# The last eight adaLN parts of a two-layer decoder: from scaling and summing to matmuls against the condition

## The chip, the cores and the metric

The kernel runs on one core of one Trainium2 chip. The metric is device time in microseconds (us) from launch to end on that core. A core has five engines that run side by side, each through its own queue in order: TensorE (PE, with its weight loads shown as PEld), VectorE (DVE), ScalarE (ACT), GpSimd (POOL) and SyncE (SP, which here only issues DMAs).

## The reference, cut to what matters

A decoder trunk of two layers over 512 tokens of 1024 features. Layer 0 mixes tokens by sparse attention, layer 1 by a gated linear recurrence (HGRN2); each mixer is followed by a mixture of 16 experts. Every one of the four sub-layers is modulated by a condition vector `c`: one product of silu(c), 1024 numbers, with a 1024 x 3072 matrix gives it a shift, a scale and a gate of 1024 numbers each.

```
cond = jax.nn.silu(c)
for layer in range(DEPTH):
    mod = jnp.einsum('bd,sde->sbe', cond, ada_w[layer]) + ada_b[layer][:, None, :]
    shift, scale, gate = jnp.split(mod[0], 3, axis=-1)
    h = rms_norm(x, norm_g[layer, 0]) * (1.0 + scale[:, None, :]) + shift[:, None, :]
    y = nsa_mixer(h, ...) if layer % 2 == 0 else hgrn2_mixer(h, ...)
    x = x + gate[:, None, :] * y
    shift, scale, gate = jnp.split(mod[1], 3, axis=-1)
    h = rms_norm(x, norm_g[layer, 1]) * (1.0 + scale[:, None, :]) + shift[:, None, :]
    x = x + gate[:, None, :] * hier_moe(h, ...)
```

All is float32. The four matrices of `ada_w` are 12 MB each, and are read once.

## The kernel before

**The parts.** `ada_parts(l, s)` cuts the matrix of a sub-layer into six parts of 512 columns, so there are 24 in all, numbered 6 * (2l + s) + t. A part is loaded as one tile `w` of 128 partitions x 8 slices x 512 columns (2 MB, line 91). Slice k holds rows 128k to 128k+127 of the matrix, and `cond[:, k]` holds the condition for them, one number for each partition. Parts 0 to 15 (`POOLED = 16`) are done on PE: for each slice and each quarter g of the columns one matmul with `cond[:, k]` spread over 32 columns as weights, into rows 32g to 32g+31 of one PSUM tile `ada_ps` (line 185). Eight such matmuls (two slices, four quarters) are one piece; the helper `side_by_side` raises the priority of all but the first and ties each to the one before, so that the scheduler queues a piece without a break. After each piece the generator yields.

Parts 16 to 23 go another way. Line 192 lets ACT multiply each of the eight slices by its condition, in place; line 198 lets POOL add the halves of the tile, 2048, 1024 and 512 columns wide; and line 202 lets PE sum over the partitions, with four matmuls against ones. Parts 16 and 17 are the gate of the HGRN2 mixer, parts 18 to 23 shift, scale and gate of the second mixture. Behind either way DVE takes the result out of PSUM (line 206 for a gate, line 209 for the others, which PE then transposes on line 211).

**The second mixer.** `hgrn` normalizes the tokens and runs `proj_stream` over eight weight tiles, called tile 0 to 7 here. ACT and DVE split each into a rounded part and a remainder (`whi`, `wlo`, lines 310 and 311) and PE multiplies: 96 matmuls of 512 columns for each tile (lines 337 to 339 and 341 to 343, `pr_ps`), the bulk of the stage. The split of the next tile happens during the last quarter of the current one. Between these matmuls the recurrence of eight heads is threaded (`hgrn_levels`, lines 1031 to 1088): nine levels, and at each PE multiplies small blocks of `Q` and `K` (`lvA_ps` to `lvD_ps`, lines 1043 to 1073), then DVE updates `Q` and `K` in place (lines 1080 and 1081), and the next level's matmuls need that. `hgrn_rest` closes a head (`ho_ps`, `ho_tp`). Only behind the last head comes the output projection (`out_ps`, lines 373 to 375) with its own two weight tiles, split on lines 313 and 314, and behind it the second mixture.

**What sets the order.** The code is traced by generators: `merge` advances the parts by 0.45 of a step (`HADA`) for each step of the heads, and `advance` the stream by 1.25 steps (`HSTREAM`). The framework's scheduler then orders the instructions of each engine, at build time, by priority and its own estimates; on the chip each engine takes them strictly in that order and waits where one is not ready. Weight tiles and parts share a ring of two buffers (`ring`, `RING = 2`): a load waits on its queue, SP's for most and POOL's for the first ones, until the tile two loads earlier is used up. The PSUM tiles of `mm_ps` (three buffers) are shared by `pr_ps`, `ada_ps` and `ho_ps`.

Of the kernel before, what the change touches and what calls it, by code (L numbers as in the profile page):

```python
# [13 lines left out]
AF = mybir.ActivationFunctionType  # L14
ALU = mybir.AluOpType
# [5 lines left out]
NK = D // 128  # L21
# [8 lines left out]
RING = 2  # L30
RINGB = 4
EARLY = 3
POOLED = 16
ADDED = 1

PARTS = ((0, 1, 2), (3,))
PINNED = (13, 14, 15)
# [25 lines left out]
def kernel(ctx: ExitStack, tc: tile.TileContext, I, out, dbg=None, upto="all"):  # L63
    nc = tc.nc
# [11 lines left out]
    def mm_ps(name):  # L76
        return psum.tile([128, 512], F32, tag="mm", bufs=3, name=name)

    def tp_ps(name):
        return psum.tile([128, 512], F32, tag="tp", bufs=3, name=name)  # L80
# [8 lines left out]
    def load_w(src, pool=ring, eng=nc.sync):  # L89
        w = pool.tile([128, 8, 512], F32, tag="w", name="w")  # L90
        loads.append(eng.dma_start(out=w, in_=src))
        return w
# [28 lines left out]
    with sb("init") as init:  # L121
# [16 lines left out]
        cond = const.tile([128, 8], F32, name="cond")  # L138
# [3 lines left out]
    def edge(ins, other, sync=False):  # L142
        tc.add_manual_dep(ins.ins, other.ins.name,
                          mybir.DependencyInfo(mybir.DependencyClass.Sync if sync else mybir.DependencyClass.NoSync,
                                               mybir.DependencyReason.DATA), reason="side by side")

    def side_by_side(makes):

        first = last = makes[0]()
        for make in makes[1:]:  # L150
            with tc.high_priority(offset=TOGETHER):
                ins = make()
            edge(ins, last)
            last = ins
        return first
# [5 lines left out]
    onef = const.tile([128, 1], F32, name="onef")  # L161
    nc.gpsimd.memset(onef, 1.0)

    def ada_parts(l, s):

        aw = I["ada_w"][l, s]
        mod = const.tile([128, 16], F32, name=f"mod{l}{s}")
        gg = const.tile([128, 2, 128], F32, name=f"gg{l}{s}")
        mods[l, s] = mod
        gates[l, s] = gg  # L170

        def load(t, wpool, eng):
            if t == 4:
                nc.gpsimd.memset(gg, 0.0)
                nc.scalar.dma_start(out=gg[0:128:32],
                                    in_=bass.AP(tensor=I["ada_b"].tensor,
                                                offset=I["ada_b"].offset + 3 * D * (2 * l + s) + 2 * D,
                                                ap=[[128, 4], [512, 2], [1, 128]]))
            return load_w(aw[:, 512 * t:512 * t + 512].rearrange("(k p) n -> p k n", p=128), wpool, eng)

        def part(t, w):
            if 6 * (2 * l + s) + t < POOLED:
                ps = mm_ps("ada_ps")
                for q in range(0, NK, 2):
                    side_by_side([lambda k=k, g=g: nc.tensor.matmul(
                        ps[32 * g:32 * g + 32, 0:128], cond[:, k:k + 1].to_broadcast([128, 32]),
                        w[:, k, 128 * g:128 * g + 128], start=(k == 0), stop=(k == NK - 1))
                        for k in (q, q + 1) for g in range(4)])
                    yield
            else:  # L190
                for k in range(NK):
                    nc.scalar.activation(w[:, k], w[:, k], AF.Copy, scale=cond[:, k:k + 1])  # L192
                    if k % 2:
                        yield
                n = NK
                while n > ADDED:
                    n //= 2
                    nc.gpsimd.tensor_tensor(w[:, 0:n], w[:, 0:n], w[:, n:2 * n], op=ALU.add)  # L198
                ps = mm_ps("ada_ps")
                for k in range(n):  # L200
                    for g in range(4):
                        nc.tensor.matmul(ps[32 * g:32 * g + 32, 0:128], onef.to_broadcast([128, 32]),
                                         w[:, k, 128 * g:128 * g + 128], start=(k == 0), stop=(k == n - 1))
                yield
            if t >= 4:
                nc.vector.tensor_add(gg[:, t - 4], gg[:, t - 4], ps[:, 0:128])
                return
            row = small.tile([128, 128], F32, tag="adarow", bufs=2, name="adarow")
            nc.vector.tensor_copy(row, ps[:, 0:128])
            tp = tp_ps("ada_tp")  # L210
            nc.tensor.transpose(tp[:, 0:128], row, ident)
            b0 = (2 * l + s) * 24 + 4 * t
            m4 = mod[:, 4 * t:4 * t + 4]
            nc.vector.tensor_add(m4, tp[:, 0:128:32], cols[:, b0:b0 + 4])
            if t >= 2:
                g0 = 96 + (2 * l + s) * 8 + 4 * (t - 2)
                nc.vector.scalar_tensor_tensor(m4, m4, 1.0, cols[:, g0:g0 + 4], op0=ALU.add, op1=ALU.mult)

        return [(lambda wpool=ring, eng=nc.sync, t=t: load(t, wpool, eng), lambda w, t=t: part(t, w)) for t in range(6)]

    def in_turn(parts, ahead, wpool=ring):
# [1545 lines left out]
```

## Time and profile before

| | us |
|---|---|
| median of 3 runs | 1475.61 |
| lowest and highest | 1474.67, 1477.06 |
| the profiled execution, own time | 1478.35 |
| its span, first to last instruction | 1476.5 |
| PE busy (share of the span) | 1291.1 (87%) |
| DVE busy | 723.1 (49%) |
| ACT busy | 468.1 (32%) |
| POOL busy | 225.5 (15%) |
| mean granted clock of PE, in parts of full speed | 0.944 |

Times inside a profile are counted from the first instruction. The span is 1.85 us shorter than the execution's own time, and the profiled execution is 2.74 us longer than the median. Busy times are unions of the instructions' own times; an engine that waits is not busy. [...] A matmul of 32-bit numbers stands as two instructions in the profile, as does its weight load.

### The profile page before, as it was taken

Reading aid. Unit: us, or ns where it says so; the run is one execution under the profiler, and the core shown is the slowest. Engines: PE = TensorE matmul, PEld = TensorE weight load, DVE = VectorE, ACT = ScalarE, POOL = GpSimd, SP = SyncE. Lnnn points to the kernel's source line nnn. Section 1 sums busy time; section 2 is a strip of 40 time slices with the busy share of each in tenths; the row PEclk is TensorE's granted clock in tenths of the full one; section 3 lists DMA queues with packets and bytes.
Section 4 is the critical chain, followed back from the end, with each engine's and each line's share of the span. In section 5 each row is a group of like instructions: output and inputs, shape, how many; then the busy total and the mean of one; then the engine's idle time right before and its main releaser. Section 6 shows DMA issues by size and latency. Waiting matters only on the chain. (4 is left out here: it accounts for less than half of the span.)

```text
span 1476.5 us, 25266 instructions
## 1 busy us (share of the span) xinstructions
PE 1291.1 (87%) x10122; PEld 767.6 (52%) x10123; DVE 723.1 (49%) x1791; ACT 468.1 (32%) x1071; POOL 225.5 (15%) x198
## 2 busy tenths in 40 slices
PE   4998899988989699999983998888979699999983
PEld 3776555765558333333323866566767543333330
DVE  2636886468854722222217476777665641222213
ACT  2523555336533211111115434344533121111110
POOL 1202212222100100000014025222130100000002
PEclk9999999999999799999996999999989799999997
DMA  9702552634564899999986222433338699999995
GB/s 354 206 11 85 176 185 91 252 121 152 192 265 157 282 368 343 376 381 334 384 325 182 86 103 87 157 115 115 115 115 299 235 343 365 360 377 335 367 397 193
DMA packets 168733, 346.42 MB, mean 235 GB/s; under 512 B 17236, under 2 KB 40620, under 8 KB 168605
## 3 DMA queue, kind: packets, MB, share of 16 engines
q1 hardware_dynamic: 135984, 276.80, 52.6%
q0 software_dynamic: 10560, 38.54, 8.0%
q10 hardware_dynamic: 22060, 29.34, 6.0%
q8 instruction: 84, 1.38, 0.4%
q14 instruction: 45, 0.36, 0.1%
HBM read 320.73 MB, written 23.93 MB: 233 GB/s over the span
## 5 line engine op out<-in xcount | busy, mean ns | idle before, releaser
L1452 PE MATMUL h_ps<-w,hgt 128*32 128x256 f32 (+1 forms) x2240 | 332.9, 488 | 0.0
L1452 PEld LDWEIGHTS h_ps<-w,hgt 128*32 128x32 f32 (+1 forms) x2240 | 111.8, 123 | 203.1 <-issue 172.4
L1479 PE MATMUL y_ps<-w,gT 128*32 128x256 f32 (+1 forms) x1120 | 163.6, 499 | 2.5 <-ACT gT L1468 2.1
L1458 DVE TENSOR_TENSOR g<-h_ps,g 32x256 f32<-32x256 f32 (+1 forms) x70 | 38.9, 556 | 253.7 <-ACT g L1456 253.1
L1456 ACT ACTIVATE g<-h_ps 64x512 f32<-64x512 f32 (+1 forms) x52 | 26.8, 516 | 368.2 <-PE h_ps L1452 346.2
L337 PE MATMUL pr_ps<-whi,hThi 128*128 128x512 f32 x288 | 119.6, 417 | 1.8 <-DVE qn L498 1.8
L338 PE MATMUL pr_ps<-wlo,hThi 128*128 128x512 f32 x288 | 115.6, 401 | 0.3 <-DVE wlo L311 0.3
L339 PE MATMUL pr_ps<-whi,hTlo 128*128 128x512 f32 x288 | 115.7, 402 | 0.2 <-DVE hTlo L283 0.2
L1479 PEld LDWEIGHTS y_ps<-w,gT 128*32 128x32 f32 (+1 forms) x1120 | 54.9, 125 | 97.3 <-issue 81.3
L1482 DVE TENSOR_TENSOR y<-y_ps,gate 128x512 f32<-128x512 f32 (+1 forms) x52 | 31.1, 598 | 123.3 <-PE y_ps L1479 107.5
L311 DVE TENSOR_TENSOR wlo<-w,whi 128x512 fp32r<-128x512 f32 x120 | 79.7, 702 | 23.0 <-ACT whi L310 22.8
L310 ACT ACTIVATE whi<-w 128x512 fp32r<-128x512 f32 x120 | 70.8, 629 | 39.0 <-SPq L1589 14.2
L782 ACT ACTIVATE P<-P,nm 128x128 f32<-128x128 f32 (+3 forms) x128 | 70.9, 556 | 36.9 <-DVE nm L780 35.8
L1416 POOL DMA_INDIRECT hg<-xnd,gidxp x26 | 23.7, 913 | 384.8 <-PE hg_tp L1428 383.0
L776 PE MATMUL s_ps<-kT,qT 128*128 128x256 f32 (+3 forms) x256 | 64.8, 358 | 12.0 <-DVE qn L498 6.9
L198 POOL TENSOR_TENSOR w<-w 128x2048 f32<-128x2048 f32 (+2 forms) x24 | 67.0, 2792 | 47.3 <-ACT w L192 46.1
L780 DVE CUSTOM_DVE_ANT_0 P<-s_ps,tb 128x128 f32<-128x128 f32 (+3 forms) x128 | 59.5, 485 | 21.5 <-PE s_ps L776 18.8
L1436 DVE TENSOR_SCALAR hgt<-hg_tp,mod 128x96 f32<-128x96 f32 (+2 forms) x128 | 43.7, 365 | 41.9 <-PE hg_tp L1428 36.4
L337 PEld LDWEIGHTS pr_ps<-whi,hThi 128*128 128x128 f32 x288 | 55.6, 193 | 15.1 <-issue 3.3
L339 PEld LDWEIGHTS pr_ps<-whi,hTlo 128*128 128x128 f32 x288 | 55.4, 192 | 12.2 <-DVE hTlo L283 0.4
L338 PEld LDWEIGHTS pr_ps<-wlo,hThi 128*128 128x128 f32 x288 | 55.9, 194 | 11.0 <-DVE wlo L311 0.7
L821 PE MATMUL p_tp<-ident,P 128*128 128x128 f32 x320 | 52.8, 282 | 8.2 <-DVE P L796 7.9
(361 smaller groups left out, 2121.9 us busy)
## 6 DMA issues: line engine op xcount, KB each, us to landing
w<-in_moe_w_dram SPq DMA_DIRECT2D x120, 1024.0 KB, 9.7
w<-in_moe_w_dram SPq DMA_DIRECT2D x32, 2048.0 KB, 9.5
w<-in_ada_w_dram SPq DMA_DIRECT2D x22, 2048.0 KB, 9.3
w<-in_hgrn_w_in_dram SPq DMA_DIRECT2D x12, 1024.0 KB, 6.9
tb<-tabd ACTq DMA_DIRECT2D x16, 456.0 KB, 3.8
yd<-y ACTq DMA_DIRECT2D x56, 128.0 KB, 5.0
w<-in_nsa_w_in_dram SPq DMA_DIRECT2D x3, 2048.0 KB, 8.1
yd<-zero POOLq DMA_DIRECT2D x12, 512.0 KB, 9.6
```

The source lines that it names most:

```text
L198: nc.gpsimd.tensor_tensor(w[:, 0:n], w[:, 0:n], w[:, n:2 * n], op=ALU.add)
L310: nc.scalar.activation(a, w[:, k], AF.Copy)
L311: nc.vector.tensor_sub(b, w[:, k], a.bitcast(F32))
L337: nc.tensor.matmul(ps, hi[:, k, c], a, start=(k == 0), stop=False)
L338: nc.tensor.matmul(ps, hi[:, k, c], b, start=False, stop=False)
L339: nc.tensor.matmul(ps, lo[:, k, c], a, start=False, stop=(k == NK - 1))
L776: nc.tensor.matmul(sp[:, :n], qT[:, (hd + j) % 8, 128 * t:128 * t + 128], kT[:, v, br, gl, :n], start=(v == 0), stop=(v == 1))
L780: nc.vector.tensor_tensor_reduce(ps, sp[:, :n], tbs[hd + j][:, 384 - 128 * t:512], scale=-1.0, scalar=3.0e38, op0=ALU.add, op1=ALU.min, ac ...
L782: nc.scalar.activation(ps, ps, AF.Exp, bias=nm[:, i:i + 1], scale=-1.0, accum_out=z[:, i:i + 1])
L821: nc.tensor.transpose(tp[:, 128 * (t - kc):128 * (t - kc) + 128], Ps[j][:, offs[t] + 128 * kc:offs[t] + 128 * kc + 128], ident)
L1452: nc.tensor.matmul(ps[m * j:m * j + m, :w], hgt[:, k, r:r + m], ws[half][:, x + i, c:c + w], start=(k == 0), stop=(k == NK - 1))
L1479: nc.tensor.matmul(ps[m * j:m * j + m, :w], gT[:, f, r:r + m], w2v[:, f, w * j:w * j + w], start=(f == 0), stop=(f == 3))
```

## The change

Parts 16 to 23 take the way of the other sixteen. The branch and its two constants go: no scaling on ACT, no sums on POOL, no matmuls against ones. Each of the eight parts becomes four pieces of eight matmuls with the condition as weights. `onef` stays, since another line uses it. A part yields four times instead of five.

```diff
-POOLED = 16
-ADDED = 1
...
         def part(t, w):
-            if 6 * (2 * l + s) + t < POOLED:
-                ps = mm_ps("ada_ps")
-                for q in range(0, NK, 2):
-                    side_by_side([lambda k=k, g=g: nc.tensor.matmul(
-                        ps[32 * g:32 * g + 32, 0:128], cond[:, k:k + 1].to_broadcast([128, 32]),
-                        w[:, k, 128 * g:128 * g + 128], start=(k == 0), stop=(k == NK - 1))
-                        for k in (q, q + 1) for g in range(4)])
-                    yield
-            else:
-                for k in range(NK):
-                    nc.scalar.activation(w[:, k], w[:, k], AF.Copy, scale=cond[:, k:k + 1])
-                    if k % 2:
-                        yield
-                n = NK
-                while n > ADDED:
-                    n //= 2
-                    nc.gpsimd.tensor_tensor(w[:, 0:n], w[:, 0:n], w[:, n:2 * n], op=ALU.add)
-                ps = mm_ps("ada_ps")
-                for k in range(n):
-                    for g in range(4):
-                        nc.tensor.matmul(ps[32 * g:32 * g + 32, 0:128], onef.to_broadcast([128, 32]),
-                                         w[:, k, 128 * g:128 * g + 128], start=(k == 0), stop=(k == n - 1))
+            ps = mm_ps("ada_ps")
+            for q in range(0, NK, 2):
+                side_by_side([lambda k=k, g=g: nc.tensor.matmul(
+                    ps[32 * g:32 * g + 32, 0:128], cond[:, k:k + 1].to_broadcast([128, 32]),
+                    w[:, k, 128 * g:128 * g + 128], start=(k == 0), stop=(k == NK - 1))
+                    for k in (q, q + 1) for g in range(4)])
                 yield
```

The first mixer and the first mixture keep their order on every engine; the first rows that differ lie in the second mixer, within its first head. Line numbers of the changed kernel are 2 lower up to the branch and 18 lower behind it. Three places show what moves.

POOL's queue at parts 16 to 18, before, behind the memory set of the gate. `rs` is the small power that closes a head:

```order
L174 MEMSET gg_111 128x256
L91 DMA w<-in_ada_w_dram 128x8x512
L198 TENSOR_TENSOR w<-w 128x2048
L198 TENSOR_TENSOR w<-w 128x1024
L198 TENSOR_TENSOR w<-w 128x512
L91 DMA w<-in_ada_w_dram 128x8x512
L1134 TENSOR_TENSOR rs_8305<-ss_8302,mhalf 128x4
L198 TENSOR_TENSOR w<-w 128x2048
L198 TENSOR_TENSOR w<-w 128x1024
L198 TENSOR_TENSOR w<-w 128x512
```

The same place after:

```order
L172 MEMSET gg_111 128x256
L89 DMA w<-in_ada_w_dram 128x8x512 x2
L1116 TENSOR_TENSOR rs_8334<-ss_8331,mhalf 128x4
L1116 TENSOR_TENSOR rs_8649<-ss_8646,mhalf 128x4
L1116 TENSOR_TENSOR rs_9000<-ss_8997,mhalf 128x4
```

All 24 sums are gone; between the two loads and the second mixture POOL keeps the eight powers alone.

PE's queue at part 16, before, with what each row waits for. This stands 2.81 tiles into the stream:

```order
L343 MATMUL pr_ps<-hTlo,whi 128x512
L1043 MATMUL lvA_ps<-Q,K 32x32 x16
L202 MATMUL ada_ps<-w,onef 32x128 [waits DMASW3_49,Activation_49,Pool_49]
L202 MATMUL ada_ps<-w,onef 32x128 x3
L341 MATMUL pr_ps<-hThi,whi 128x512
```

After, 2.25 tiles into the stream, the part's first two pieces:

```order
L1025 MATMUL lvA_ps<-q,K 32x32 x15
L1025 MATMUL lvA_ps<-Q,K 32x32 x16
L182 MATMUL ada_ps<-w,cond 32x128 [waits DMASW3_49]
L182 MATMUL ada_ps<-w,cond 32x128 x7
L323 MATMUL pr_ps<-hThi,whi 128x512
L324 MATMUL pr_ps<-hThi,wlo 128x512
L325 MATMUL pr_ps<-hTlo,whi 128x512
L323 MATMUL pr_ps<-hThi,whi 128x512
L324 MATMUL pr_ps<-hThi,wlo 128x512
L325 MATMUL pr_ps<-hTlo,whi 128x512
L182 MATMUL ada_ps<-w,cond 32x128 x8
```

The part moved forward by half a tile, its matmuls went from four in one place to thirty-two in four, and the first of them now waits for the load itself, where POOL's sum stood between before.

PE's queue at the end of the stream, before, behind the last tile's last matmul: the eighth head's first two sets of blocks and the seventh head's end:

```order
L339 MATMUL pr_ps<-whi,hTlo 128x512
L1043 MATMUL lvA_ps<-q,K 32x32 x16
L1043 MATMUL lvA_ps<-Q,K 32x32 x16
L1124 MATMUL ho_ps<-vS,AD 128x128 [waits DVE_49]
L1124 MATMUL ho_ps<-vS,AO 128x128
```

After, the place where tile 7 begins, one tile earlier:

```order
L1025 MATMUL lvB_ps<-Q,K 32x32 x15
L1025 MATMUL lvA_ps<-q,K 32x32 [waits DVE_49,PE_49]
L1025 MATMUL lvA_ps<-q,K 32x32 x15
L1025 MATMUL lvA_ps<-Q,K 32x32 x5
L1025 MATMUL lvB_ps<-Q,K 32x32 [waits DVE_49]
L1025 MATMUL lvB_ps<-Q,K 32x32 x15
L1025 MATMUL lvA_ps<-Q,K 32x32 x11
L182 MATMUL ada_ps<-w,cond 32x128 [waits DMAHW1_49]
L182 MATMUL ada_ps<-w,cond 32x128 x7
L319 MATMUL pr_ps<-whi,hThi 128x512
```

The eighth head's first two sets of blocks (`q`, then `Q`) moved ahead of the whole last tile. So did part 23, which before stood with part 22 some rows behind the seventh head's end; its first piece waits for the load and stands ahead of the tile's first matmul.

## Rows read from the trace of the kernel before

**Rows 1.** Busy us of each engine, granted clock, DMA share and GB/s, by stretches

```profile
850.00:1080.00 230.00, 203.81 (x2302) 155.75 (x2302) 162.38 (x310) 98.51 (x190) 71.28 (x31) 0.94 0.33 111
...
1080.00:1110.00 30.00, 21.69 (x313) 17.65 (x313) 23.07 (x42) 11.52 (x21) 5.94 (x4) 0.77 0.44 159
...
1190.00:1440.00 250.00, 244.20 (x1780) 92.12 (x1774) 54.77 (x136) 41.85 (x97) 9.88 (x11) 0.99 1.01 364
```

**Rows 2.** Groups by line, 850 to 1080: busy us, mean ns | idle before, releaser

```profile
L198 POOL TENSOR_TENSOR w<-w 128x2048 f32<-128x2048 f32 (+2 forms) x23 | 65.6, 2855 | 47.3 <-ACT w L192 46.1
...
L192 ACT ACTIVATE w<-w,cond 128x512 f32<-128x512 f32 x64 | 41.1, 714 | 13.6 <-DVE adarow L209 5.5 <-DMA w<-in_ada_w_dram 4.3 <-DVE Q L1080 3.1
```

**Rows 3.** Instructions by time, 1024 to 1036: start, us, engine, line [idle before <-releaser]

```profile
1025.78 8.45 POOL L198 TENSOR_TENSOR w<-w 128x2048 f32<-128x2048 f32 x3 [7.74 <-ACT w L192]
...
1025.88 4.76 DVE L1081 TENSOR_TENSOR K<-K,Tc 128x256 f32<-128x256 f32 x1
...
1026.85 0.39 PE L342 MATMUL pr_ps<-hThi,wlo 128*128 128x512 f32 x1
1027.08 0.40 PE L343 MATMUL pr_ps<-hTlo,whi 128*128 128x512 f32 x1
...
1030.70 0.68 PE L1063 MATMUL lvC_ps<-Q,K 128*64 128x64 f32 x8 [3.22 <-DVE K L1081]
```

**Rows 4.** Line 1081 alone, 840 to 1080: ns min/median/max, first and last start

```profile
L1081 DVE TENSOR_TENSOR K<-K,Tc x49: 410/418/4759, 852.9 to 1064.8; 128x256 f32<-128x256 f32 x49
```

**Rows 5.** PE by time, 866 to 1085: the waits of over 1 us beside that of Rows 3

```profile
870.36 0.73 PE L1068 MATMUL lvC_ps<-Q,K 128*128 128x128 f32 x4 [3.39 <-DVE K L1081]
...
899.27 1.12 PE L1063 MATMUL lvC_ps<-Q,K 128*64 128x64 f32 x8 [3.52 <-DVE K L1081]
...
915.76 0.43 PE L1043 MATMUL lvA_ps<-Q,K 128*32 128x32 f32 x28 [2.04 <-DVE K L1081]
...
959.67 0.55 PE L1043 MATMUL lvB_ps<-Q,K 128*32 128x32 f32 x24 [6.17 <-DVE K L1081]
...
994.85 0.38 PE L1057 MATMUL lvB_ps<-Q,K 128*32 128x32 f32 x6 [4.26 <-DVE K L1081]
...
1035.76 0.49 PE L1068 MATMUL lvC_ps<-Q,K 128*128 128x128 f32 x2 [1.43 <-DVE K L1081]
...
1083.80 0.46 PE L1043 MATMUL lvA_ps<-Q,K 128*32 128x32 f32 x32 [1.58 <-DVE K L1081]
```

**Rows 6.** Stretches, as Rows 1, of half clock between 850 and 1080: sum of the five

```profile
sum 27.31, PE 21.38 PEld 16.31 DVE 22.13 ACT 3.58 POOL 12.85; mean PE 4.28 PEld 3.26 DVE 4.43 ACT 0.72 POOL 2.57
```

**Rows 7.** PE by time: a piece in the first mixer, the sum over partitions in the second

```profile
352.06 0.64 PE L185 MATMUL ada_ps<-w,cond 128*32 128x128 f32 x16
352.63 0.50 PE L776 MATMUL s_ps<-kT,qT 128*128 128x256 f32 x2
...
878.49 0.45 PE L202 MATMUL ada_ps<-w,onef 128*32 128x128 f32 x8
878.87 0.50 PE L341 MATMUL pr_ps<-hThi,whi 128*128 128x512 f32 x1
```

**Rows 8.** Line 185, 50 to 800: ns min/median/max; then all its waits (us, times)

```profile
L185 PEld LDWEIGHTS ada_ps<-w,cond x768: 105/110/177, 147.4 to 396.7; 128*32 128x32 f32 x192
...
  issue: 8.7, 32
  DVE nm L780: 1.2, 3
  DVE z L784: 0.3, 2
```

**Rows 9.** Loads of parts, 850 to 1080: count, KB, median us from issue to landing

```profile
w<-in_ada_w_dram SPq DMA_DIRECT2D x6, 2048.0 KB, 8.0
...
w<-in_ada_w_dram POOLq DMA_DIRECT2D x2, 2048.0 KB, 9.1
```

**Rows 10.** By time: SP's load of part 22 where tile 7 has been split

```profile
1049.36 8.92 SPq L91 DMA_DIRECT2D w<-in_ada_w_dram  x2
```

**Rows 11.** PE by time: the first output projection matmul behind the last head

```profile
1098.29 0.79 PE L373 MATMUL out_ps<-whi,ohi 128*128 128x512 f32 x1 [1.34 <-ACT whi L313]
```

## The prediction

> **What bounds the kernel now.** I read the busy times by stretches first [rows 1]. The changed parts lie between 850 and 1080, in the second mixer. There PE is busy 203.8 of 230 us, so the order of its queue carries the stage, and 26.2 us of it are waits. Behind it comes a stretch that is full as well: from 1190 to 1440 PE is busy 244 of 250 us and the DMA engines all the time. The second mixture thus has nothing to catch up with, and a shift of the mixer's end moves the kernel's end by as much.
>
> Next, what the removed work does in that stretch, by groups of lines [rows 2]: POOL sums for 65.6 us (a 24th sum lies just behind), ACT scales for 64 x 0.714 = 45.7 us. Neither engine is near its limit. Their price is elsewhere, and the instructions by time show it [rows 3]: POOL starts its sums at 1025.78, DVE starts the next `K` update at 1025.88 and ends it 4.76 us later, and PE, which needs that `K`, stands for 3.22 us. The same update lasts 0.418 us in the median and 4.759 us at most [rows 4]. PE's waits for the `K` of line 1081 of more than 1 us are eight [rows 3, 5], and at each one of POOL's sums runs against the update. They are 3.39 + 3.52 + 2.04 + 6.17 + 4.26 + 3.22 + 1.43 + 1.58 = 25.6 us. Seven lie before 1080 and make 24.0 of the 26.2 us; without the sums PE would hardly wait in this stretch.
>
> After the long ones the granted clock is at 0.5 for a while. There are five such stretches between 850 and 1080, 27.31 us in all, in which PE works 21.38 us [rows 6]. The 2.04 us wait at 915.76 has no such stretch behind it, the ones of 3.22 us and more all have.
>
> **The change part by part.** *Sums and scaling go.* The eight waits fall away as far as nothing else is late: the updates return to 0.42 us, and between the waits the same chain of PE and DVE runs covered by projection matmuls. Credit: 25.6 us. ACT's 45.7 us are worth nothing directly, since outside the seven waits PE stands for only 2.2 us.
>
> *The clock comes back.* 21.38 us of work at half clock take 10.7 us at full clock. Credit: 10.7 us. Both credits hang on the same cause and fall together.
>
> *Thirty-two pieces come onto PE.* The first mixer has the same piece: it starts at 352.06 and what follows at 352.63, 0.57 us for eight matmuls in sixteen instructions [rows 7]. The four matmuls against ones take 0.38 us for eight instructions [rows 7], so by that row a piece would be 0.76 us. I take 0.57, the same instructions in the same shape: 32 x 0.57 = 18.2 us. The eight old bursts go, 8 x 0.38 = 3.0 us. Debit: 15.2 us, at most 21.3. PE's queue is the path here, so all of it counts. POOL and ACT hid this work from PE's own queue; that cover is gone.
>
> [...] A piece's weight loads last 0.110 us each [rows 8], yet sixteen of them and sixteen matmul instructions pass in 0.57 us [rows 7], so they overlap. [...] All matmuls of a piece use all rows. [...]
>
> *The pieces wait for their loads.* Before, ACT stood at the load and PE's matmul came with POOL's sums between. Now PE's queue stands, and with it the projection and all heads' levels behind the piece. A part lands 8.0 us after issue from SP, 9.1 from POOL [rows 9], and is issued when the ring gives a buffer free. For parts 18, 20, 21 and 22 the order puts about 28 to 54 projection matmuls, one every 0.23 us [rows 3], and the levels between them between release and piece: over 8 us, no wait. For 16, 17 and 19 it is 24 to 31, and with the levels some 8 to 9 us: a wait of 0 to 1.5 us each. Part 23 is the tight one. Its load can go only when tile 7 has been split, which before is 1049.36 [rows 10] and lands at 1057.4, about 9 us behind the place where tile 7 begins. The changed order has only levels of two heads, the end of one and two pieces there, about 7 us, with no projection matmul between them as cover. I take 5 us for this place, with the clock, and 1 for the rest. Debit: 6 us; 0 if all is landed, 18 if five parts wait 3 us and the clock drops.
>
> In the first mixer twelve parts go this way, and among the waits of their line there is none for a load [rows 8]. There attention lies between; here the ring also carries the projection's tiles.
>
> *Behind the last head.* Its first two sets of blocks move ahead of the last tile. Before, the next set is at 1083.80, 3.4 us behind the stream's end, of which 1.58 are already counted [rows 5]; about 1.9 us remain. Parts 22 and 23 release the ring earlier, so the output weights come earlier, and the wait of 1.34 us for them [rows 11] can go. Against it, their subtractions may now stand among the head's updates on DVE: eight of them on 512 columns, 5.7 us if each takes the 0.714 us of ACT's scaling of that size [rows 2]. I take a credit of 2.5 us, from 3.2 to a debit of 2.5.
>
> *At nothing:* DVE's work behind a part is the same. SP's loads are the same in number; one part's load moves ahead of a tile's, which by the order is released in time. `ada_ps` holds one of three PSUM buffers longer, four pieces instead of one burst; the third case has its price.
>
> The sum: -25.6 - 10.7 + 15.2 + 6.0 - 2.5 = **-17.6 us**. The profiled execution took 1478.35 us, which gives 1460.7. It is 2.74 us above the median of the runs, so the forecast for the median is **1458 us**.
>
> **The rivals.** *First, the forecast:* POOL's grip on DVE is the cost, PE's new work the price. With its own terms at their ends, 1451 (no load waited for, the tail at its best: -24.3) to 1470 (pieces of 0.76 us and 12 us of waits: -5.5).
>
> *Second, slower: PE stands for the loads.* The place is the first piece of each part at the head of PE's queue. Without waits the change is worth 17.6 + 6 = 23.6 us, so the sign turns at 23.6 / 8 = 2.95 us of wait for each part. With 4 us each, half of a landing, it is +32 - 23.6 = +8.4: 1484 us. For it: part 23, the ring's two buffers, and a stream that runs faster now while a load does not. Against it: the distances above and the first mixer.
>
> *Third, no change: the waits return in another form.* With the sums gone the heads' chain may meet another limit, such as a projection piece that lacks a PSUM buffer while `ada_ps` and a head's `ho_ps` hold two of three, or levels without cover. If half of both credits goes, 18.2 us, it is +0.6: 1476 us. Against it: between the eight waits PE stands for only those 2.2 us in the stretch.
>
> [...]
>
> That the change doesn't do what it says can be left aside: the order shows no sum and no scaling any more.
>
> **How the numbers follow.** The forecast has 0.78, the second case 0.09, the third 0.10, the fourth 0.02, and 0.01 is left. A measurement of this kernel can tell about 0.2%, 3 us, from no change. All of the forecast's range is faster; of the third I count 0.03 as faster and 0.07 as the same, with the 0.01 left; the second and fourth are slower: 0.81, 0.08, 0.11. The range reaches from 1449, a little below the forecast's lower end, to 1474, where the third case begins, which takes in its better part.
>
> **What would show it.** Right: POOL's busy time falls by about 67 us and ACT's by about 45; the longest update of line 1081 is near 0.42 us while no sum runs; the eight waits for `K` are gone, and with them the half-clock stretches in the stage; a piece takes 0.57 us; from the mixture on, all stands about 18 us earlier. Wrong: PE waits named for `w<-in_ada_w_dram` at `ada_ps`, above all where tile 7 begins, of more than 3 us each; new waits of PE for DVE or ACT in the places of the old; pieces of over 0.76 us; or a mixture that starts earlier and ends at the same time.

## The result, and the profile after

| | before | after |
|---|---|---|
| median, us | 1475.70 | 1458.72 |
| lowest and highest | 1474.67, 1477.06 | 1455.70, 1461.93 |
| runs | 4 | 4 |
| profiled execution, own time | 1478.35 | 1461.16 |
| its span | 1476.5 | 1459.3 |
| POOL busy | 225.5 | 157.9 |
| ACT busy | 468.1 | 429.6 |
| DVE busy | 723.1 | 690.7 |

The ratio is 0.9885, with a 95% interval from 0.9857 to 0.9913: the changed kernel is 17 us faster. The forecast was 1458 us.

The stretches of [rows 1], now of the changed kernel (busy us of PE, PEld, DVE, ACT and POOL, each with its instructions, then granted clock, DMA share, GB/s):

```profile
850.00:1080.00 230.00, 218.79 (x2973) 167.90 (x2972) 141.61 (x334) 67.89 (x140) 8.35 (x8) 0.97 0.38 129
1080.00:1110.00 30.00, 26.80 (x136) 21.32 (x136) 18.38 (x30) 8.41 (x17) 1.01 (x1) 0.93 0.59 213
...
1190.00:1440.00 250.00, 238.59 (x1692) 89.20 (x1688) 52.82 (x111) 38.57 (x91) 12.73 (x14) 0.99 0.99 355
```

Between 850 and 1080 PE now waits 11.2 us in the place of 26.2, although it has 670 instructions more to do there, and POOL's 71 us have shrunk to 8. The clock rises from 0.94 to 0.97. The update of `K` (line 1063 now, by duration: minimum, median, maximum in ns) answers [rows 4]:

```profile
L1063 DVE TENSOR_TENSOR K<-K,Tc x56: 414/418/424, 852.0 to 1083.1; 128x256 f32<-128x256 f32 x56
```

Its longest is 0.424 us; before it was 4.759. The new price stands in two groups of PE's instructions and in the waits before them (busy, mean ns | idle before, releaser):

```profile
L319 PE MATMUL pr_ps<-whi,hThi 128*128 128x512 f32 x96 | 41.8, 435 | 1.0 <-DVE on L1119 0.9
...
L182 PE MATMUL ada_ps<-w,cond 128*32 128x128 f32 x512 | 21.1, 282 | 2.7 <-DMA w<-in_ada_w_dram 2.6
```

The first row shows a small new wait: once, for 0.9 us, a projection matmul has no PSUM buffer until DVE has read a head's end (line 1119 reads `ho_ps`).

The place where tile 7 begins is the one that the prediction called tight. PE by time there, and then the stretch of half clock behind it:

```profile
1034.64 0.46 PE L1025 MATMUL lvB_ps<-Q,K 128*32 128x32 f32 x32 [1.47 <-DVE ss L1114]
...
1037.86 1.08 PE L182 MATMUL ada_ps<-w,cond 128*32 128x128 f32 x16 [1.11 <-DMA w<-in_ada_w_dram]
1038.87 0.80 PE L319 MATMUL pr_ps<-whi,hThi 128*128 128x512 f32 x1
```

```profile
1036.40:1043.23 6.83, 5.72 (x54) 4.28 (x44) 2.15 (x6) 0.00 (x0) 0.00 (x0) 0.50 0.81 297
```

PE stands twice there, 1.47 and 1.11 us, the second time for part 23's load, and the clock is at 0.50 for 6.83 us. It falls at 1036.40, after the first stand and 0.35 us before the second begins (1037.86 - 1.11 = 1036.75). All other waits for a part's load are at most 1.02 us.

### The profile page after: what moved, and what is told of

Same layout as the page of the kernel before. It is cut to its first block, busy times and chain, and to the rows that moved or that the text cites. A ratio compares the mean times of both kernels' runs of the same rounds, so it can differ in the third digit from the quotient of the medians.

```text
span 1459.3 us, 26081 instructions
## 1 busy us (share of the span) xinstructions
PE 1294.2 (89%) x10570; PEld 770.2 (53%) x10571; DVE 690.7 (47%) x1791; ACT 429.6 (29%) x1007; POOL 157.9 (11%) x174
## 5 line engine op out<-in xcount | busy, mean ns | idle before, releaser
L292 ACT ACTIVATE whi<-w 128x512 fp32r<-128x512 f32 x120 | 71.9, 631 | 44.8 <-SPq L1571 15.8
L182 PE MATMUL ada_ps<-w,cond 128*32 128x128 f32 x1536 | 63.8, 297 | 14.4 <-DMA w<-in_ada_w_dram 14.2
```

Source lines behind the costliest of these rows:

```text
L182: side_by_side([lambda k=k, g=g: nc.tensor.matmul(ps[32 * g:32 * g + 32, 0:128], cond[:, k:k + 1].to_broadcast([128, 32]), w[:, k, 128 * g ...
L292: nc.scalar.activation(a, w[:, k], AF.Copy)
```

## The experiments

Each time below is the median of its runs; the ratio is to the kernel before on the same chip. The experiments ran on three chips, on which the kernel before took 1475.76 to 1478.14 us. Differences between two experiments of under about 4 us are within their intervals. Where a difference is smaller, the traces are compared, one execution each: from the first matmul of tile 0 to PE's last. The first matmul stands between 793 and 800 us (815 in the last experiment, which changes what lies ahead), so the part ahead of it, which is the same code, by itself varies by some 6 us.

**Were POOL's sums the cost?** Four kernels ask this. The first is the kernel before without them:

```diff
-                    nc.gpsimd.tensor_tensor(w[:, 0:n], w[:, 0:n], w[:, n:2 * n], op=ALU.add)
```

> The kernel before without POOL's 24 sums: parts 16 to 23 then take only the first of their eight slices, so that 7/8 of these eight products are left out; ACT's scaling, the loads and the four matmuls against ones stay where they are. Theory (POOL's sums hold DVE's updates of K, PE waits for those, and the clock falls behind the waits): the longest update of line 1081 falls from 4.76 to about 0.42 us, the eight waits of 25.6 us go, and with them most of the half clock in the stage (10.7 us of work): 1475.6 - 25.6 - 10.7 = about 1439 us (1433 to 1447). Rival (the waits lie in the order of PE's queue or in the part's place in it, and the sums only happen to run beside them): PE still waits for K, and the time stays above 1465 us. If only the waits go and the clock falls anyway: about 1450 us.

Measured: 1439.55 us, ratio 0.9734 (0.9713 to 0.9755). The update of `K` in this kernel:

```profile
L1080 DVE TENSOR_TENSOR K<-K,Tc x56: 416/418/422, 853.0 to 1063.7; 128x256 f32<-128x256 f32 x56
```

The theory holds: PE has the same instructions to do, the eight waits are gone, and the time is the one expected. On its own chip the kernel before took 1478.14 us, so that the sums cost 38.6 us there, 2.3 more than the 36.3 of the theory. The second keeps the computation whole and moves the sums to PE:

```diff
-ADDED = 1
+ADDED = 8
```

> The kernel before with ADDED = 8: no sums on POOL, but ACT's scaling stays, and a part is 32 matmuls against ones at one place of PE's queue, not tied into pieces. Theory: what pays is the absence of the sums, and the price is 32 matmuls for a part, whatever their weights: -36.3 for waits and clock, +15.2 for the matmuls: about 1455 us (1448 to 1463), some us below the changed kernel if its waits for loads are worth anything. Rival (the unbroken pieces with the condition and their places are what pays): nearer to 1475 than to 1459 us. If 32 matmuls in one place leave the heads' levels waiting behind them, new waits of PE for DVE, or of DVE for PE, of about 2 us for each part: 1470 us.

Measured: 1445.60 us, ratio 0.9782 (0.9759 to 0.9805): below the range of the theory, and 13 us below the changed kernel. No expectation had that; the next group of runs is on it. The third goes the other way and gives POOL adds that nobody needs, in the changed kernel:

```diff
         nc.gpsimd.tensor_tensor(rs[:, 0:NT], ss[:, 0:NT], mhalf.to_broadcast([128, NT]), op=ALU.pow)
+        z = idle[0]
+        nc.gpsimd.tensor_tensor(z[:, 0:NT], ss[:, 0:NT], ss[:, 0:NT], op=ALU.add)
+        for n in (1024, 1024, 1024, 512):
+            nc.gpsimd.tensor_tensor(z[:, 0:n], z[:, 0:n], z[:, 0:n], op=ALU.add)
```

> The changed kernel, with work put back on POOL that nobody needs: behind each head's small power one tiny add that takes the same input, then four adds of a scratch tile to itself (three of 1024 columns, one of 512), some 8.6 us a head at the durations of the sums of before. PE's order is word for word that of the changed kernel, and no engine waits for the scratch tile. Theory (an add on POOL stops DVE's updates in SBUF for as long as one add lasts, up to 2.4 us here): updates of 2 to 3 us on lines of Q and K, new waits of PE for K, half clock behind the longer ones: 12 to 36 us above the changed kernel, 1471 to 1495 us, likeliest about 1478. Rival (POOL's sums cost through the semaphores and the part's own chain, not through DVE): within 0.2% of 1458.7 us.

Measured: 1494.01 us, ratio 1.0100 (1.0076 to 1.0124), 35 us above the changed kernel: at the upper end of the theory's range, 16 us above its likeliest value. The fourth puts memsets in the place of the adds, which in sum last somewhat longer (9.04 us against 7.40 for a head). There are two cases: that POOL is busy is enough, or DVE is stopped by adds and not by memsets, and the time stays that of the changed kernel:

```diff
-        for n in (1024, 1024, 1024, 512):
-            nc.gpsimd.tensor_tensor(z[:, 0:n], z[:, 0:n], z[:, 0:n], op=ALU.add)
+        for n in range(9):
+            nc.gpsimd.memset(z, 0.0)
```

> As the run before, but the four adds are nine memsets of 1024 columns, some 8.5 us a head at 0.94 us each: POOL is busy just as long and only writes. If POOL's being busy is enough, as with the adds: 12 to 36 us above the changed kernel. [...] I expect the second, with 0.7.

Measured: 1458.74 us, ratio 0.9871 (0.9836 to 0.9905): the time of the changed kernel, the second case. The same place in the two kernels, behind the first head's power, tells why. With adds (start, us, engine, line; the last two rows are from a later head):

```profile
883.38 0.69 DVE L1127 TENSOR_TENSOR on<-ho_ps,rs 128x512 f32<-128x512 f32 x1 [0.57 <-POOL rs L1120]
883.60 7.40 POOL L1124 TENSOR_TENSOR idle<-idle 128x1024 f32<-128x1024 f32 x4
884.10 1.93 DVE L1128 TENSOR_TENSOR on<-on,gS 128x512 f32<-128x512 f32 x1
885.96 2.11 DVE L1064 TENSOR_TENSOR Q<-Q,Tc 128x256 f32<-128x256 f32 x1
887.99 2.11 DVE L1065 TENSOR_TENSOR K<-K,Tc 128x256 f32<-128x256 f32 x1
...
890.15 0.66 PE L1027 MATMUL lvB_ps<-Q,K 128*32 128x32 f32 x32 [4.77 <-DVE K L1065]
...
985.90 7.41 POOL L1124 TENSOR_TENSOR idle<-idle 128x1024 f32<-128x1024 f32 x4
...
992.33 0.68 DVE L1085 TENSOR_TENSOR mk<-lvA_ps,cst 128x512 f32<-128x512 f32 x1
```

With memsets:

```profile
881.36 0.69 DVE L1127 TENSOR_TENSOR on<-ho_ps,rs 128x512 f32<-128x512 f32 x1 [0.57 <-POOL rs L1120]
881.56 9.04 POOL L1124 MEMSET idle<- 128x1024 f32 x9
882.09 0.69 DVE L1128 TENSOR_TENSOR on<-on,gS 128x512 f32<-128x512 f32 x1
882.70 0.42 DVE L1064 TENSOR_TENSOR Q<-Q,Tc 128x256 f32<-128x256 f32 x1
883.03 0.42 DVE L1065 TENSOR_TENSOR K<-K,Tc 128x256 f32<-128x256 f32 x1
```

Under the adds, four in 7.40 us, each DVE operation on two inputs from SBUF lasts 1.93 to 2.11 us: three of them stand in a row, and PE waits 4.77 us for the third. An operation with one input from PSUM (`lvA_ps`, at 992.33) lies wholly under such a burst and keeps its 0.68 us. Under the memsets, which only write, the same three keep 0.69, 0.42 and 0.42 us. So it is not that POOL is busy: 7.40 us of adds lengthen all three, 9.04 us of memsets none. Under the adds the two `Q` and `K` updates last 2.11 us each, about as long as one add of 1024 columns (1.98 us in the mean between 840 and 1080), and under the memsets 0.42. The adds read SBUF and the memsets don't; that it is the reading which stops DVE fits these rows, but no run shows it apart.

**Why is 32 against ones 13 us better?** Four runs vary the place of the matmuls and their cutting. The first lets each of the last eight parts wait four steps and then run whole:

```diff
+            late = 6 * (2 * l + s) + t > 15
+            for _ in range(4 if late else 0):
+                yield
...
-            for q in range(0, NK, 2):
+            step = NK if late else 2
+            for q in range(0, NK, step):
...
-                    for k in (q, q + 1) for g in range(4)])
+                    for k in range(q, q + step) for g in range(4)])
```

> The changed kernel, but a part of the last eight first lets four steps pass and is then 32 matmuls with the condition in one unbroken run: the places of the run before with 32 matmuls against ones (2.81, 3.69, 4.56 tiles into the stream and so on), without ACT's scaling. Open is why that run, at 1445.6 us, is 13 us faster than the changed kernel though both put 32 matmuls of a part onto PE and none of the sums onto POOL. If it is the place (behind the load, and nothing of the last parts ahead of tile 7): 1446 us (1441 to 1451). If it needs ACT's scaling between load and matmuls, as a cover for the load: PE waits named for the load, 1452 to 1460 us. If matmuls against ones are cheaper than those against the condition: about 1458 us.

Measured: 1447.84 us, ratio 0.9802 (0.9775 to 0.9828). So neither the weights nor ACT's scaling explain the 13 us: with the condition as weights, no scaling, and the same places, the time is within the intervals that of the run with ones (624.3 us by the trace, 626.3 with ones). In the trace no matmul of a part waits for a load any more, and a whole part is one run of 64 instructions:

```profile
872.44 1.97 PE L186 MATMUL ada_ps<-w,cond 128*32 128x128 f32 x64
874.34 0.50 PE L327 MATMUL pr_ps<-hThi,whi 128*128 128x512 f32 x1
```

The second moves the four steps behind the run:

```diff
-            for _ in range(4 if late else 0):
-                yield
...
-                yield
+                for _ in range(4 if late else 1):
+                    yield
```

> As the run before, but the four steps pass behind the 32 matmuls: they stand in one run where the changed kernel has a part's first piece (2.25, 2.81, 3.56 and so on; part 23 where tile 7 begins). If the place costs the 13 us: waits for the load at several parts and at tile 7, 1455 to 1466 us. If it is the cutting into four pieces with the projection and the levels between them: 1445 to 1450 us.

Measured: 1452.86 us, ratio 0.9846 (0.9823 to 0.9870), between the two expectations. The fourth corner is four pieces, but later:

```diff
-HADA = 0.45
+HADA = 0.36
```

> The changed kernel with HADA = 0.36 in the place of 0.45. A part now yields four times in the place of five, so 0.36 gives it the pace over the heads' steps that it had before; the pieces stand later, part 22 across the end of the stream and part 23 among the last head's levels. If the waits for loads, the half clock where tile 7 begins and the bare tail cost what the prediction and the trace of after say (some 4 us of waits, 3.4 of clock, about 5 in the tail): 1450 us (1446 to 1454). If the pieces cost the same wherever they stand: 1458.7 us within 0.2%.

Measured: 1451.94 us, ratio 0.9847 (0.9829 to 0.9865), within the first expectation. The four corners (median us; the three others were timed on one chip, the change apart from them):

| | four pieces | one run |
|---|---|---|
| early | 1458.7 (the change) | 1452.9 |
| late | 1451.9 | 1447.8 |

By the traces they are 637.6 (the change), 632.0 (one run, early), 630.1 (four pieces, late) and 624.3 us (one run, late), so the two effects add: later places are worth 7.5 to 7.7 us, whole runs 5.6 to 5.8.

Why the later places pay can be read from the stretch of the stream and the one behind it, up to the last output matmul, here with four pieces and late (columns as above):

```profile
842.60:1055.40 212.80, 208.45 (x2675) 157.75 (x2667) 133.22 (x312) 60.05 (x128) 8.30 (x8) 1.00 0.36 120
```

```profile
1055.42:1132.43 77.01, 70.64 (x661) 58.04 (x661) 47.93 (x84) 27.84 (x47) 3.69 (x5) 0.98 0.66 239
```

In the changed kernel the two take 220.20 us at a clock of 0.98 and 76.53 at 0.93 (their rows stand in the next section). The stream becomes 7.4 us shorter: some 160 instructions of PE have left it, it waits 2.1 us less and it has no half clock. The stretch behind it takes those instructions up for 0.5 us: PE waits less there, 6.4 us in the place of 8.0, and has more of the full clock, 0.98 in the place of 0.93.

Is the second the price of each cut? This was tried by cutting finer:

```diff
-HADA = 0.45
+HADA = 0.90
...
-            for q in range(0, NK, 2):
+            step = 1 if late else 2
+            for q in range(0, NK, step):
```

> The changed kernel with each of the last eight parts in eight pieces of four matmuls in the place of four of eight; HADA is doubled to 0.90, so that a part's eight steps pass over the same stretch of the heads as its four before. If each cut of PE's stream costs by itself (a piece between two projection matmuls adds 0.78 us by the trace of after, of which 0.57 is the piece): 32 cuts more by 0.2 us, +6.4, 1465 us. By the four runs on place and cutting (four pieces in the place of one cost 5.7 us, 24 cuts): +7.6, 1466 us. If what the four pieces cost is not the cuts but the wait and the half clock where tile 7 begins: 1457 to 1460 us.

Measured: 1464.67 us, ratio 0.9927 (0.9901 to 0.9952). The number is the one expected of the cuts, the reason only half so. The stream from tile 2's first matmul to the last, here and in the run whole and early, and two stretches of half clock in the former (same columns as above):

```profile
843.60:1071.30 227.70, 218.86 (x2836) 162.49 (x2828) 134.22 (x315) 61.48 (x128) 7.87 (x8) 0.98 0.36 122
```

```profile
846.20:1058.20 212.00, 207.80 (x2790) 162.64 (x2776) 131.97 (x315) 60.93 (x128) 8.25 (x8) 1.00 0.41 140
```

```profile
875.57:878.98 3.41, 3.41 (x14) 1.99 (x15) 0.45 (x1) 0.63 (x1) 0.00 (x0) 0.50 0.02 5
1039.41:1046.24 6.83, 6.06 (x87) 3.98 (x87) 2.70 (x7) 0.00 (x0) 0.00 (x0) 0.50 0.87 316
```

Take PE's busy time in the stream less half of what ran at half clock, an estimate of its work at full clock: 218.86 - 4.74 = 214.1 us in eight pieces, 213.74 - 2.86 = 210.9 in four, 207.8 in one. Some pieces came to stand side by side, so that by the traces the stream holds 55, 30 and 8 separate runs of such matmuls. The 25 cuts from four to eight cost 3.2 us, the 22 from one to four 3.1, so a cut costs an estimated 0.13 to 0.14 us. What else the step from four to eight costs is waits, 8.84 us in the stream against 6.46, and one more stretch of half clock: with four pieces there is only the one at tile 7. And one run in the place of four pieces shortens the stream by 8.2 us: 3.1 of cuts, 2.3 of waits, 2.9 of half clock at tile 7; 2.6 of it are lost again behind the stream. So the cuts themselves are the smaller part; the larger is waits and half clock, which changed with the order of the pieces.

What a piece costs was measured apart, by making it twice:

```diff
+            n = 2 if 6 * (2 * l + s) + t > 15 else 1
-            for q in range(0, NK, 2):
+            for i, q in enumerate(list(range(0, NK, 2)) * n):
...
-                yield
+                if i % n == n - 1:
+                    yield
```

> The changed kernel with every piece of the last eight parts twice: a part's product is made once, thrown away and made again, in the same four places, so that 32 pieces more of eight matmuls pass through PE's queue and nothing else changes. Price of a piece by the prediction, 0.57 us: +18.2, 1477 us. By the spacing of an unbroken run of 32, 1.98 us: 0.495 us each, +15.8, 1474.5 us. [...] Below +10 us: pieces lie partly in waits that are there anyway.

Measured: 1470.21 us, ratio 0.9966 (0.9948 to 0.9984), 11.5 us above the changed kernel, 0.36 us for each piece more. That is less than the forecasts by either price, and more than the 10 us below which pieces would lie in waits. In the trace a doubled piece and what follows it:

```profile
854.87 1.08 PE L183 MATMUL ada_ps<-w,cond 128*32 128x128 f32 x32 [0.75 <-DMA w<-in_ada_w_dram]
855.88 0.50 PE L325 MATMUL pr_ps<-hThi,whi 128*128 128x512 f32 x1
```

From start to start it takes 1.01 us against 0.57 for one, 0.44 more, which makes 14.1 us for 32. Nearly 3 us of that come back by the traces: the stream has 1.6 us less of waits, and a shorter stretch of half clock where tile 7 begins (3.41 us there, 6.83 in the changed kernel). If the sixteen loads of a piece passed one by one, with no matmul beside them, a piece would take an estimated 16 x 0.110 + 0.57 = 2.33 us [rows 7, 8], the prediction's fourth case, and 32 more of them 74.6 us: that is out.

**Two versions that should have been better.** Whole late parts, with more of them behind the stream:

```diff
-HADA = 0.45
+HADA = 0.36
```

> Whole late parts (as the run of that name, 1447.8 us) with HADA = 0.36: parts 21, 22 and 23 then stand behind the stream's end, among the last head's levels, in the place of two. If a part there fills PE's waits for K and keeps the clock up (4.6 us of waits and 6.83 us of half clock are left in that place): 1444 us (1441 to 1447). If the output projection's weights, which follow the parts in the ring, then come late: 1449 to 1456 us.

Measured: 1457.31 us, ratio 0.9853 (0.9818 to 0.9888), 9.5 us worse than with 0.45 (12.0 by the traces), a miss. Two places take it. One is tile 3, where the weights of tile 4 come late, by time (ACT, DVE, PE):

```profile
896.68 0.63 ACT L296 ACTIVATE whi<-w 128x512 fp32r<-128x512 f32 x1 [6.68 <-DMA w<-in_hgrn_w_in_dram]
...
897.35 0.69 DVE L297 TENSOR_TENSOR wlo<-w,whi 128x512 fp32r<-128x512 f32 x1 [4.30 <-ACT whi L296]
...
898.29 0.42 DVE L1067 TENSOR_TENSOR K<-K,Tc 128x256 f32<-128x256 f32 x1
...
898.76 0.79 PE L1059 MATMUL lvD_ps<-Q,K 128*128 128x256 f32 x1 [3.96 <-DVE K L1067]
```

Here a late load of weights stops PE through two queues: ACT stands 6.68 us for it, DVE 4.30 for ACT's half of the split, and PE 3.96 for the update of `K` queued behind that split. The matmul behind that wait lasts 0.79 us, where those of its kind last 0.424 in the mean, and between 850 and 1080 the granted clock is 0.97, 0.99 in the run with 0.45. Part 17's load on POOL's queue and the tile's two on SP's ran together there, and these two took 14.6 us to land, where the median of such loads in the changed kernel is 6.8:

```profile
w<-in_ada_w_dram POOLq DMA_DIRECT2D x1, 2048.0 KB, 10.4
w<-in_hgrn_w_in_dram SPq DMA_DIRECT2D x2, 1024.0 KB, 14.6
```

The other place is the last head: from the stream's end to the first output matmul it takes 23.3 us in the place of 16.8, one part more and a wait of 3.23 us for its load among them. Three parts there were too many in this order; two whole parts there (1447.84) were better than none (1452.86).

The last run makes the first sixteen parts whole and late as well:

```diff
-            late = 6 * (2 * l + s) + t > 15
+            late = True
```

> Whole late parts, and the first sixteen parts in the same way: four steps, then 32 matmuls in one run. If a cut costs PE's stream 0.2 us wherever it stands: 16 x 3 x 0.2 = 9.6 us less at most, less what of it lies in waits of the first mixer, so 1439 to 1446 us. If PE isn't the bound where these parts stand: 1447.8 us within 0.2%.

Measured: 1466.32 us, ratio 0.9931 (0.9902 to 0.9961), a miss by over 20 us. The second mixer and what follows take as long as without this (625.4 against 624.3 us), but tile 0 starts 16.3 us later. Nearly all of it arises in the first mixer, where twelve of the first sixteen parts stand. The first mixer in this kernel, from 130 us to the end of its last transpose of attention weights (`p_tp`; columns as above), and one group of PE's instructions there:

```profile
130.00:431.40 301.40, 263.85 (x2018) 182.64 (x2016) 195.30 (x575) 141.59 (x419) 61.07 (x59) 0.93 0.43 148
```

```profile
L762 PE MATMUL s_ps<-kT,qT 128*128 128x256 f32 (+3 forms) x256 | 68.8, 372 | 18.1 <-DVE qn L484 6.9 <-DVE nm L766 6.4 <-ACT qT L540 3.5
```

The same two in the changed kernel, whose first sixteen parts are in four pieces each:

```profile
130.00:415.90 285.90, 255.91 (x2018) 172.79 (x2016) 196.11 (x579) 142.82 (x418) 61.68 (x59) 0.98 0.46 159
```

```profile
L758 PE MATMUL s_ps<-kT,qT 128*128 128x256 f32 (+3 forms) x256 | 66.0, 364 | 11.7 <-DVE qn L480 6.9 <-DVE nm L762 4.2 <-DVE sc L716 0.3
```

The same 2018 instructions take 15.5 us more: 7.6 us of waits (37.6 against 30.0), and 7.9 us of work at a lower clock (0.93 against 0.98). Attention makes PE wait for DVE and ACT. That small pieces among these waits cover them, and that a whole run covers one and leaves the others bare, fits the rows; no run shows it apart.

The version to keep is thus the change with whole late runs for the last eight parts alone (1447.84 us), or the kernel before with `ADDED = 8` (1445.60 us); the two intervals overlap. Both lie below that of the change.

## Why the prediction was right, by its steps

The run without sums splits the change in two: from before to it lies the credit, from it to the changed kernel the debit. The three kernels in three stretches, from tile 2's first matmul to the stream's last, from there to the last output matmul, and to PE's last. Before:

```profile
848.48:1080.40 231.92, 205.73 (x2322) 156.85 (x2314) 163.90 (x312) 99.35 (x192) 72.35 (x31) 0.94 0.33 110
1080.40:1159.98 79.58, 70.09 (x565) 57.91 (x564) 49.30 (x84) 27.71 (x47) 7.18 (x7) 0.91 0.63 232
1159.98:1453.20 293.22, 272.32 (x1943) 106.81 (x1941) 80.23 (x262) 50.14 (x114) 20.93 (x23) 0.95 0.97 348
```

Without sums:

```profile
848.50:1048.50 200.00, 196.06 (x2322) 149.91 (x2315) 132.32 (x312) 98.75 (x192) 8.27 (x8) 1.00 0.38 128
1048.50:1126.20 77.70, 69.46 (x565) 57.35 (x565) 47.78 (x85) 27.73 (x47) 4.09 (x5) 0.93 0.65 237
1126.20:1418.10 291.90, 270.47 (x1942) 106.23 (x1940) 80.00 (x262) 50.06 (x114) 20.68 (x23) 0.96 0.97 349
```

After:

```profile
847.50:1067.70 220.20, 213.74 (x2834) 163.33 (x2828) 133.49 (x315) 61.02 (x128) 7.86 (x8) 0.98 0.37 126
1067.70:1144.23 76.53, 68.56 (x500) 56.24 (x501) 46.94 (x81) 27.70 (x47) 4.05 (x5) 0.93 0.58 213
1144.23:1436.30 292.07, 270.27 (x1942) 106.06 (x1940) 80.24 (x262) 50.04 (x114) 20.84 (x23) 0.96 0.98 349
```

| step | predicted | measured | how |
|---|---|---|---|
| waits for `K` go | -25.6 | -23.5 | stretch less PE busy, first two stretches: 26.2 + 9.5 before, 3.9 + 8.2 without sums |
| clock comes back | -10.7 | -10.3 | PE busy, first two: 205.73 + 70.09 before, 196.06 + 69.46 without sums |
| the pieces | +15.2 | +14.8 | PE busy of the stream, 213.74 - 196.06, less 2.9 for half clock |
| waits for loads, with clock | +6.0 | +5.4 | waits of the stream, 6.5 - 3.9, and the 2.9 |
| behind the last head | -2.5 | -1.2 | second stretch, 77.70 to 76.53 |
| the mixture | 0 | -1.2 | third stretch, 293.22 to 292.07 |
| sum | -17.6 | -16.0 | |

The profiled execution itself became 17.2 us shorter. The 1.2 us that the table lacks lie outside its stretches: tile 2 starts 1.0 us earlier, though the code ahead of it is the same, and some 0.3 lie behind PE's last matmul. From the second mixture on, all stands 15.8 us earlier, where the prediction said about 18.

*The credit* was right in cause and size. The clock's share is confirmed by a kernel that has 3.9 us of waits in the stream in the place of 26.2: without sums the granted clock is 1.00 there, 0.94 before, and the same 2322 instructions take 196.06 us of PE in the place of 205.73.

*The pieces* came within half a microsecond, although the row that priced them leaves something out. PE by time, a piece between two projection matmuls of the changed kernel:

```profile
858.95 0.40 PE L325 MATMUL pr_ps<-hTlo,whi 128*128 128x512 f32 x1
859.28 0.64 PE L182 MATMUL ada_ps<-w,cond 128*32 128x128 f32 x16
859.85 0.50 PE L323 MATMUL pr_ps<-hThi,whi 128*128 128x512 f32 x1
860.19 0.39 PE L324 MATMUL pr_ps<-hThi,wlo 128*128 128x512 f32 x1
```

The piece takes its 0.57 us, but the step ahead of it and the one behind it take 0.33 and 0.34 in the place of 0.23, so that in such a place it adds 0.78. Next to the levels' small blocks it adds less (0.48 at 975.60: from the start of the blocks to the next projection matmul 0.87 us, where without a piece, at 886.57, it is 0.39), and 31 pieces in the stream, with six old bursts gone, average near to the price taken. That they do is in part luck, and so is the size of the row: it also holds the eighth head's first two sets of blocks, 64 instructions that moved into the stream from behind it, about 0.7 us by their starts without sums.

*The waits for loads* were right in place and near in sum, most of it at tile 7 as forecast (1.47 + 1.11 us of waits and 2.9 of half clock, 5.4 for the 5 taken); but the parts of it are not those of the prediction. Part 16 makes PE wait 1.02 us, part 20, which was thought safe, 0.49; parts 17 and 19, thought doubtful, nothing worth naming. The turning point of the second rival, 2.95 us for each part, was far off. At tile 7 the load alone makes 1.11 us. The other 1.47 are a wait for DVE that the prediction did not name, though PE could not have passed part 23's piece before its load was there in any case. The half clock is not the load's doing by these rows: it begins at 1036.40, 0.35 us before PE stands for the load. What brought the clock down was not tested; that the sum is right is in part luck.

*The tail* is where the prediction was too hopeful, by about 1 us: the wait for the output weights is gone as forecast, but the eighth head still has three bare waits for `K` there, 0.96, 1.54 and 2.26 us, and 10.24 us at half clock.

*"At nothing"* held but for the 0.9 us in which a projection matmul waited for a head's `ho_ps`: the third rival's mechanism is there, at a twentieth of the price that it would need. With the 1.47 us for DVE at tile 7, a wait in another form too, it is an eighth. ACT's busy time fell by 38.5 us and not by 45: the eight scalings overlap (41.1 us busy where 64 of them sum to 45.7 [rows 2]), and nobody waited for them.

What the prediction lacked is the third possibility, that the sums can go and the pieces' place be better than in the change. It priced the path that the change takes, nearly rightly, and didn't ask what part of its own debit of 21 us was needed: 6 to 8 of the 19 were.

## What to carry to other kernels

An engine with a third of its time in use (POOL, 71 of 230 us) set the pace here, since its operations stopped those of another that lie on the critical chain: compare the longest of an operation with its median (4.759 us with 0.418 here), and look at what ran beside the long ones. Work that was moved onto an engine with hardly any idle time was best placed, in this kernel, where its input had long landed and in one run (1447.84 us, 1458.72 in the change); where the engine waited for others in short gaps, the same work did better in small pieces (1447.84 us, 1466.32 with whole runs there as well). So both forms are worth a try in each stage. And a wait removed was worth more than its length here, since the clock had fallen beside the waits (0.94 in the stream, 1.00 without the sums): 10 us on top of 24.

## What the runs showed of the hardware

- A stop is about as long as one operation of POOL: under its adds of 1024 columns (1.98 us in the mean) DVE operations on two SBUF inputs lasted 1.93 to 2.11 us in the place of 0.42 to 0.69, one after another. An operation that took an input from PSUM kept its time (0.68 us at 992.33, under a burst), and memsets on POOL stopped no update of `K`: beside 63 of them between 840 and 1080 the longest lasted 0.424 us.
- Sixty-four matmul instructions of this shape (thirty-two matmuls), each with weights over all rows, pass in 1.90 us from their start to that of the next matmul (872.44 to 874.34), though a load of such weights lasts 0.110 us and 64 of them would take 7.0. So the loads do not pass one by one with no matmul beside them, here as little as in [rows 7, 8]. Such matmuls stand as two instructions each; a projection matmul, whose operands are rounded, stands as one (768 for the 768 of the eight tiles, before).
- Where a piece stands between two projection matmuls, the step to it and the step behind it are some 0.10 us longer than between two projection matmuls (0.33 and 0.34 against 0.23). A cut of a run costs an estimated 0.13 to 0.14 us in this stream, where most pieces have a level's small blocks on one side.
